# PEER gates of the first 64 tokens: accumulating indirect DMAs into a DRAM grid in place of one-hot products, in a two-block transformer step on one Trainium2 core

## The chip, the cores and the metric

The kernel runs on one core of one Trainium2 chip. The metric is the device time of one execution in microseconds. The core has five engines with instruction queues of their own: TensorE (PE in the profile; PEld is its weight load), VectorE (DVE), ScalarE (ACT), GpSimd (POOL) and SyncE (SP, which here only issues DMAs).

## What is computed

256 tokens of width 1024 pass through two blocks: a first one (gated linear attention beside sparse attention, cross attention, a PEER feed-forward), a second one (a gated recurrence beside long convolutions, a PEER feed-forward), with norms between. The change touches the PEER layer alone, which stands in both blocks:

```python
q = (xt @ wq).reshape(N, H, 2, PEER_DKEY // 2)
s = jnp.einsum('nhpd,hpkd->nhpk', q, subkeys).astype(jnp.float32)
s_half, i_half = lax.top_k(s, K)                      # 8 heads, 16 of 128 keys, twice
cand_s = (s_half[:, :, 0, :, None] + s_half[:, :, 1, None, :]).reshape(N, H, K * K)
cand_i = (i_half[:, :, 0, :, None] * PEER_NKEYS + i_half[:, :, 1, None, :]).reshape(N, H, K * K)
top_s, pos = lax.top_k(cand_s, K)
eidx = jnp.take_along_axis(cand_i, pos, axis=-1)
gate = jax.nn.softmax(top_s, axis=-1)
...
act = jax.nn.gelu(jnp.einsum('cd,chkd->chk', xc, down[ec])) * gc
y = jnp.einsum('chk,chkd->cd', act, up[ec])
```

Each token picks 8 x 16 experts of 128 x 128, and an expert's number is a pair (i, j) of key indices. The kernel does not gather experts. It computes all 16384 hidden values of all tokens, multiplies them by a gate that is zero for the experts not picked, and multiplies by all of `up`. An expert that several heads of one token pick has the sum of their gates.

## The kernel before

Matrices are streamed. `load` (244) issues one 512 KB DMA on SP's queue into one of four `wf` buffers, and `after` keeps these loads in order. `stream` (257) splits the weights: ACT copies the rounded part to `wh` (263), DVE subtracts it to get the rest, `wl` (270); both have three buffers, so they run up to three tiles ahead of PE. `mm3` (286) makes three matmuls of each pair of split operands (289 to 291). A scheduler orders each engine's instructions by readiness and by the order of the code, so DVE's order is not that of the source.

`peer` (1041) runs one PEER layer. First come the query products (`lin_t` on `wq`). `routing` (864) works on two halves of 128 tokens: the two searches for 16 keys, the search among 256 candidates, the index arithmetic, and the softmax, which ends in the multiply of line 940. Its steps are interleaved with the first 64 tiles of `down` (989), with `paced` (1032) tying them to the weight splits. One tile of `down` is 24 matmuls of 256 columns and yields the hidden values of the 128 experts of one j, for 256 tokens: row j of `H`, whose halves are `Ha` and `Hb`. ACT's gelu writes them.

The other 62 tiles (with two left for the end) are interleaved with `gate` (951), here called the gate stage. A group of four tokens takes, for each token, a one-hot matrix of its j indices times its gates (ACT, 976) and a product with the one-hot matrix of its i indices (PE, 977), which sums gates of experts picked twice. DVE multiplies the result into those columns of `H` that hold gelus already (983); where a tile of `down` comes later than the group, ACT copies the gates into `H` (985) and the tile multiplies its gelu into them (1002). DVE builds the one-hot matrices for eight tokens at a time (963). `at` is the pair that tells how many tiles and how many tokens are through.

Then `up` (1016) takes 128 pieces, one for each j: `halves` (1008) splits row j of `H` into `ah` (ACT) and `al` (DVE), in two buffers each, and 12 matmuls of 512 columns add its product with the streamed `up` weights to four accumulators.

Between the layers stands `between` (1342), a chain of residual sum, squares on ACT and two norms, whose powers are on POOL (1363). Beside it the constants of block 2 are loaded (`parts`, 427). POOL does little else: a few weight splits and products, and the powers of the norms (327).

Of the kernel before, what the change touches and what calls it, by code (L numbers as in the profile page):

```python
# [23 lines left out]
T = 256  # L24
# [3 lines left out]
NEG = -1e30  # L28
NBANK = {"lin": 3, "bank": 4, "aux": 1}
# [27 lines left out]
def _constants():  # L57
    c = {}
    c["ident"] = np.eye(P, dtype=np.float32)
    c["iota"] = np.broadcast_to(np.arange(P, dtype=np.float32), (P, P))  # L60
# [151 lines left out]
class _Kernel:  # L212
    def __init__(self, tc, ctx, A):
        self.tc, self.nc, self.A = tc, tc.nc, A
        e = ctx.enter_context
        self.pc = e(tc.tile_pool(name="const", bufs=1))
        self.px = e(tc.tile_pool(name="xs", bufs=1))
        self.pw = e(tc.tile_pool(name="w", bufs=1))
        self.ps = e(tc.tile_pool(name="ps", bufs=1, space=PSUM))
        self.dr = e(tc.tile_pool(name="dr", bufs=1, space=DRAM))  # L220
        self.small = e(tc.tile_pool(name="small", bufs=4))
        self.alt = 0
        self.last = None
        self.ahead = 3
        self.los = []

# [17 lines left out]
    def load(self, src, n):  # L244
# [4 lines left out]
        self.last = d  # L249
        return wf  # L250

# [142 lines left out]
    def setup(self):  # L394
# [4 lines left out]
        with self.tc.tile_pool(name="iota", bufs=1) as p:  # L399
            iota = self.const("iota", [P, P], pool=p)  # L400
            nc.vector.tensor_copy(self.iota, iota)
        self.mhalf = self.pc.tile([P, 1], F32, name="mhalf")
# [461 lines left out]
    def routing(self, pool, qT, sk, split_tiles, res):  # L864
# [4 lines left out]
        for i in range(2):  # L869
# [70 lines left out]
            nc.vector.tensor_tensor(out=g, in0=g, in1=sm[:, :, None].to_broadcast([P, 8, 16]), op=ALU.mult)  # L940
            b = self.bank([P, 3, P])
            for w in range(3):
                nc.tensor.transpose(b[:, w], fin[:, w].rearrange("p h k -> p (h k)"), self.ident)
# [7 lines left out]
    def gate(self, H, res, oh, at):  # L951
# [16 lines left out]
        nxt = list(hot(0))[-1]  # L968
        for t0 in range(0, T, N):
            (e, a), more = nxt, iter(hot(t0 + N)) if t0 + N < T else iter((None, None))  # L970
            for t4 in (0, 4):
# [14 lines left out]
                at[1] = t0 + t4 + 4  # L986
                yield 1

    def down(self, w, js, x, H, pool, at):
        nc = self.nc  # L990
        for j in js:
# [7 lines left out]
            if t > 0:  # L999
                g = pool.tile([P, T], F32, name="act", tag="ah")  # L1000
                nc.scalar.activation(g[:, :t], o[:, :t], AF.Gelu_apprx_tanh)
                nc.vector.tensor_tensor(out=hj[:, :t], in0=g[:, :t], in1=hj[:, :t], op=ALU.mult)
            if t < T:
                nc.scalar.activation(hj[:, t:], o[:, t:], AF.Gelu_apprx_tanh)
# [3 lines left out]
    def halves(self, hj, pool, tag, pool_lo):  # L1008

        ah = pool.tile([P, T], F32R, name="ah", tag=tag)  # L1010
# [5 lines left out]
    def up(self, w, H, pool, acc, first):  # L1016
        def piece(j):
            w2 = self.stream(w[j])
            return j, w2, first if j == 0 else self.halves(H[j // 64][:, j % 64], pool, "ah", pool)
# [21 lines left out]
    def peer(self, x, wq, nq, skname, dn, up, gain):  # L1041
        nc, A, tc = self.nc, self.A, self.tc
        with ExitStack() as st:
# [7 lines left out]
            at = [0, 0]  # L1051
            with tc.tile_pool(name="prt", bufs=1) as rp:
# [5 lines left out]
                route = self.paced(self.routing(rp, qT, sk, nq == 16, res), 1)  # L1058
# [5 lines left out]
            _interleave(self.down(A[dn], range(64, P - 2), x, H, pa, at), self.gate(H, res, oh, at), 1.02)  # L1064
            first = self.halves(H[0][:, 0], pi, "g2", pa)
# [6 lines left out]
            _run(self.up(A[up], H, pa, acc, first))  # L1072
# [319 lines left out]
    def build(self):  # L1392
        tc = self.tc
        with tc.tile_pool(name="h1", bufs=1) as ph:
# [5 lines left out]
            with tc.tile_pool(name="xap", bufs=1) as p:  # L1400
# [6 lines left out]
                self.cross(mkT, mv, self.mem_k(mc, mkT, range(6, 8)), self.mem_v(mc, mv))  # L1407
            x = self.peer_in(3)
        h, acc, g = self.peer(x, "p1_wq", 8, "p1_sk", "p1_dn", "p1_up", "nfin")
        with tc.tile_pool(name="h2", bufs=1) as ph:  # L1410
            self.h = ph.tile([P, 2, D], F32, name="hmid")
            with tc.tile_pool(name="b2n", bufs=1) as pn:
# [3 lines left out]
                self.to_cols(xn, x, range(8), lambda c: self.gains[:, 32 + c:33 + c])  # L1416
            self.block2_mix(x)
            x = self.peer_in(5)
        self.finish(*self.peer(x, "p2_wq", 16, "p2_sk", "p2_dn", "p2_up", "nfin2"))
# [22 lines left out]
```

## Time and profile before

| | |
|---|---|
| three runs, median (lowest to highest) | 2384.3 us (2381.0 to 2387.03) |
| the profiled execution, its own time | 2381.52 us |
| its span in the trace | 2379.7 us |
| mean granted clock of TensorE, share of full speed | 0.993 |
| PE, DVE, ACT, POOL busy | 98%, 71%, 54%, 3% |
| moved by DMA | 395 MB, 166 GB/s |

A line of the trace gives a start, a duration, an engine, the source line and the operation with what it writes and reads; what stands in brackets is the idle time of that engine just before and the work that ended it. PE overlaps its matmuls, so the time that one takes on PE's path is the distance of two starts, or its share in the chain of waits, and not its own duration.

### The profile page before, as it was taken

What the parts mean: (1) busy time and instruction counts of PE and PEld (TensorE: products, weight loads), DVE (VectorE), ACT (ScalarE), POOL (GpSimd) and SP (SyncE); (2) the same over time, 40 slices, a digit from 0 to 9 for tenths busy, and PEclk for the clock granted to TensorE, in tenths of its full rate; (3) what the DMA queues carried; (4) which work ended last, traced back from release to release, by engine and by line L of the source; (5) the groups of instructions that cost most, each with busy time, mean ns of one, the idle gap of its engine ahead of it and who ended that gap; (6) DMA issues with size and microseconds to landing.
All of it is one profiled execution on the core that took longest, in us unless ns stands there. A gap on an engine that the chain in (4) does not pass through costs nothing.

```text
span 2379.7 us, 40910 instructions
## 1 busy us (share of the span) xinstructions
PE 2334.1 (98%) x15646; PEld 2127.5 (89%) x15646; DVE 1686.6 (71%) x3138; ACT 1282.6 (54%) x2526; POOL 59.7 (3%) x67
## 2 busy tenths in 40 slices
PE   8999999999999999999899999999999999999998
PEld 6977889999999888888899999899999999888886
DVE  6686469886777655655778886679976777555555
ACT  6565445556777444544654434445457776444444
POOL 0002000000000000000100000200000000000000
PEclk9999999999999999999999999999999999999999
DMA  7433455564444665665554444656554444656654
GB/s 234 135 120 105 148 161 176 171 191 148 140 141 138 206 190 186 187 190 187 181 176 129 151 152 132 197 167 185 163 183 142 143 141 166 190 188 193 186 188 140
DMA packets 116084, 395.39 MB, mean 166 GB/s; under 512 B 14587, under 2 KB 21936, under 8 KB 114736
## 3 DMA queue, kind: packets, MB, share of 16 engines
q1 hardware_dynamic: 115888, 392.79, 52.7%
q8 instruction: 122, 2.00, 0.3%
q14 instruction: 74, 0.61, 0.1%
HBM read 386.45 MB, written 5.77 MB: 165 GB/s over the span
## 4 chain that ended last, share of the span: by engine, by line
PE 87%; DVE 9%; issue 1%; ACT 1%; POOL 1%; DMA 0%; POOLq 0%; SPq 0%; ACTq 0%
PE lin L291 15%; PE lin L289 15%; PE lin L290 15%; PE bank L291 10%; PE bank L289 10%; PE bank L290 10%; PE bank L977 5%; DVE wl L270 3%; PE bank L1240 1%; ACT wh L263 1%; DVE cand L906 0%; PE bank L365 0%; PE bank L655 0%; DVE pos L908 0%; PE bank L774 0%
## 5 line engine op out<-in xcount | busy, mean ns | idle before, releaser
L270 DVE TENSOR_TENSOR wl<-wf,wh 128x1024 fp32r<-128x1024 f32 (+1 forms) x698 | 852.8, 1223 | 295.7 <-ACT wh L263 295.5
L263 ACT CAST wh<-wf 128x1024 fp32r<-128x1024 f32 x704 | 735.2, 1045 | 599.0 <-PE lin L290 477.5
L289 PE MATMUL lin<-xch,wh 128*128 128x256 f32 x2912 | 839.1, 288 | 0.1
L291 PE MATMUL lin<-xch,wl 128*128 128x256 f32 x2912 | 827.5, 284 | 2.5 <-DVE wl L270 2.4
L290 PE MATMUL lin<-xcl,wh 128*128 128x256 f32 x2912 | 826.1, 284 | 0.0
L291 PEld LDWEIGHTS lin<-xch,wl 128*128 128x128 f32 x2912 | 559.1, 192 | 4.2 <-DVE wl L270 4.1
L289 PEld LDWEIGHTS lin<-xch,wh 128*128 128x128 f32 x2912 | 560.6, 193 | 2.3 <-ACT xch L375 0.7
L290 PEld LDWEIGHTS lin<-xcl,wh 128*128 128x128 f32 x2912 | 559.8, 192 | 0.0
L289 PE MATMUL bank<-wh,ah 128*128 128x512 f32 x1024 | 404.3, 395 | 0.0
L291 PE MATMUL bank<-wh,al 128*128 128x512 f32 x1024 | 404.3, 395 | 0.0
L290 PE MATMUL bank<-wl,ah 128*128 128x512 f32 x1024 | 404.2, 395 | 0.0
L291 PEld LDWEIGHTS bank<-wh,al 128*128 128x128 f32 x1024 | 192.6, 188 | 46.1
L290 PEld LDWEIGHTS bank<-wl,ah 128*128 128x128 f32 x1024 | 192.6, 188 | 45.8
L289 PEld LDWEIGHTS bank<-wh,ah 128*128 128x128 f32 x1024 | 192.6, 188 | 45.6
L976 ACT ACTIVATE c<-e,g 128x128 f32<-128x128 bf16 x512 | 175.1, 402 | 0.0
L1011 ACT CAST ah<-Hb 128x256 fp32r<-128x256 f32 x128 | 52.0, 406 | 182.4 <-PE bank L290 182.4
L1011 ACT CAST ah<-Ha 128x256 fp32r<-128x256 f32 x128 | 52.0, 406 | 177.7 <-PE bank L290 175.2
L983 DVE TENSOR_TENSOR Ha<-bank,Ha 128x256 f32<-128x256 f32 x128 | 54.2, 423 | 123.8 <-PE bank L977 119.1
L977 PE MATMUL bank<-c,a 128*128 128x128 f32 x1024 | 134.1, 274 | 0.0
L977 PEld LDWEIGHTS bank<-c,a 128*128 128x128 f32 x1024 | 124.9, 192 | 0.0
L1013 DVE TENSOR_TENSOR al<-Hb,ah 128x256 fp32r<-128x256 f32 x128 | 54.4, 425 | 78.8 <-ACT ah L1011 77.5
L1013 DVE TENSOR_TENSOR al<-Ha,ah 128x256 fp32r<-128x256 f32 x128 | 54.4, 425 | 76.0 <-ACT ah L1011 75.7
(412 smaller groups left out, 2467.2 us busy)
## 6 DMA issues: line engine op xcount, KB each, us to landing
wf<-in_p_dn_dram SPq DMA_DIRECT2D x256, 512.0 KB, 3.6
wf<-in_p_up_dram SPq DMA_DIRECT2D x256, 512.0 KB, 3.5
wf<-in_w2t_dram SPq DMA_DIRECT2D x64, 512.0 KB, 3.5
wf<-in_p_wq_dram SPq DMA_DIRECT2D x24, 512.0 KB, 3.7
wf<-in_w_out_dram SPq DMA_DIRECT2D x16, 512.0 KB, 4.2
wf<-in_w2k_dram SPq DMA_DIRECT2D x16, 512.0 KB, 3.6
wf<-in_w1t_dram SPq DMA_DIRECT2D x12, 512.0 KB, 5.0
wf<-in_w1k_dram SPq DMA_DIRECT2D x8, 512.0 KB, 3.7
```

The lines of the kernel that those rows point to most:

```text
L263: hi = self.hi = nc.scalar.copy(wh[:, :n], wf[:, :n]).ins
L270: lo = eng.tensor_tensor(out=wl[:, :n], in0=wf[:, :n], in1=wh[:, :n].bitcast(F32), op=ALU.subtract).ins
L289: mm(out, a[0], b[0], start=start, stop=False)
L290: mm(out, a[0], b[1], start=False, stop=False)
L291: self.mm = mm(out, a[1], b[0], start=False, stop=stop).ins
L976: nc.scalar.mul(c[:, x], e[:, t4 + x], gf[:, t0 + t4 + x:t0 + t4 + x + 1])
L977: nc.tensor.matmul(b[:, :, x], a[:, t4 + x], c[:, x], start=True, stop=True)
L983: nc.vector.tensor_tensor(out=hv[:, :n], in0=bv[:, :n], in1=hv[:, :n], op=ALU.mult)
L1011: self.nc.scalar.copy(ah, hj)
L1013: self.nc.vector.tensor_tensor(out=al, in0=hj, in1=ah.bitcast(F32), op=ALU.subtract)
L1240: nc.tensor.matmul(b[:, h].rearrange("p (b w m) -> p b w m", w=2, m=m), A[:, h, i * P:i * P + P], q, start=True, stop=True)
```

## The change

The 64 first tokens (`NS`) no longer take part in `gate`, which now runs from token 255 down to 64. Their gates go another way:

- `grid` makes a DRAM array of 128 x 128 x 64 numbers (i, j, token; 4 MB) for each layer. It is zeroed by eight DMAs of 512 KB from a tile of zeros, one after each of the next eight `load`s: those of the query weights for the first layer, those of the constants and first weights of block 2 for the second.
- In the first half of `routing`, two DVE operations make a table of addresses (`at`, 64 tokens x 128 picks), and `scatter` issues 128 indirect DMAs on POOL's queue, one for each pick, which add the 64 gates of this pick to the grid. Those of one head wait for all of the head before it; within a head no address repeats.
- In `up`, the grid is read back in pieces of 128 x 512 (eight j, 256 KB) on SP's queue, and `halves` multiplies the 64 columns of row j of `H` by its gates on DVE before it splits the row. The first read stands before the last two tiles of `down` in the code and waits for the last head's DMAs.
- The ratio of groups to tiles falls from 1.02 to 0.78, which spreads 48 groups over the 62 tiles.

```diff
@@ load @@
         self.last = d
+        next(self.blank, None)
         return wf
+    def grid(self, name):
+        G = self.dr.tile([P * P * NS, 1], F32, name=name)
+        v = G.rearrange("(p x) o -> p (x o)", p=P)
+        n = P * NS // 8
+        def blanks():
+            for x in range(8):
+                d = self.nc.sync.dma_start(v[:, x * n:x * n + n].rearrange("p (a t) -> p a t", t=T),
+                                           self.zero[:, None, :].to_broadcast([P, n // T, T])).ins
+                self.after(d, self.last)
+                self.last = d
+                yield x
+        self.blank = blanks()
+        return G, v
+    def scatter(self, G, at, g):
+        tc = self.tc
+        heads = self.heads[G.name] = [[]]
+        for h in range(8):
+            wait, new = heads[-1], []
+            for q in range(h * 16, h * 16 + 16):
+                d = self.nc.gpsimd.indirect_dma_start(G[:, :], bass.IndirectOffsetOnAxis(ap=at[:, q:q + 1], axis=0),
+                                                      g[0:NS, q:q + 1], None, compute_op=ALU.add).ins
+                tc.declare_no_dep(d, group=G.name, keep=wait, reason="other elements")
+                for p in wait:
+                    self.behind(d, p)
+                tc.add_to_no_dep_group(G.name, d)
+                new.append(d)
+            heads.append(new)
+    def gates(self, G, j, pool):
+        g = pool.tile([P, 8, NS], F32, name="gt")
+        d = self.nc.sync.dma_start(g.rearrange("p j t -> p (j t)"), G[1][:, j * NS:j * NS + 8 * NS]).ins
+        if j == 0:
+            for p in self.heads[G[0].name][-1]:
+                self.behind(d, p)
+        self.after(d, self.last)
+        self.last = d
+        return g
@@ routing @@
+            if i == 0:
+                at = keep.tile([NS, P], U32, name="at")
+                row = pool.tile([NS, P], F32, name="row")
+                nc.vector.tensor_scalar(row, ij[0][0:NS], float(P * NS), self.tcol[0:NS], op0=ALU.mult, op1=ALU.add)
+                nc.vector.scalar_tensor_tensor(out=at, in0=ij[1][0:NS], scalar=float(NS), in1=row, op0=ALU.mult, op1=ALU.add)
+                self.scatter(G[0], at, g)
@@ gate @@
-        nxt = list(hot(0))[-1]
-        for t0 in range(0, T, N):
+        nxt = list(hot(T - N))[-1]
+        for t0 in range(T - N, NS - 1, -N):
@@ halves @@
+        self.nc.vector.tensor_tensor(out=hj[:, :NS], in0=hj[:, :NS], in1=g, op=ALU.mult)
@@ up @@
             w2 = self.stream(w[j])
+            if j % 8 == 0 and j + 8 < P:
+                gt.append(self.gates(G, j + 8, pool))
@@ peer @@
-            _interleave(self.down(A[dn], range(64, P - 2), x, H, pa, at), self.gate(H, res, oh, at), 1.02)
-            first = self.halves(H[0][:, 0], pi, "g2", pa)
+            _interleave(self.down(A[dn], range(64, P - 2), x, H, pa, at), self.gate(H, res, oh, at), 0.78)
+            g0 = self.gates(G, 0, pa)
+            first = self.halves(H[0][:, 0], g0[:, 0], pi, "a0", pa), g0
```

Three places of the order in which the scheduler leaves the instructions. Line numbers are those of the kernel in question; in the new one 325 is the weight split (270 before), 1030 the one-hot matrices (963), 1050 the products with `H` (983), 1069 the gelus' products (1002), 1076 the new multiply, 265 a blank, 299 a read of the grid (`gt`), 250 a weight load (247).

POOL's queue from the weight splits of the first PEER layer to the powers of `between`, before:

```order
L270 TENSOR_TENSOR wl<-wf,wh 128x1024 x2
L327 TENSOR_TENSOR rstd<-rstd,mhalf 128x1 x2
L270 TENSOR_TENSOR wl<-wf,wh 128x1024
L1363 TENSOR_TENSOR ssh<-ssh,mhalf 128x1
L1363 TENSOR_TENSOR ssy<-ssy,mhalf 128x1
```

And in the changed kernel:

```order
L325 TENSOR_TENSOR wl<-wf,wh 128x1024 x2
L382 TENSOR_TENSOR rstd<-rstd,mhalf 128x1 x2
L325 TENSOR_TENSOR wl<-wf,wh 128x1024
L287 DMA gates_3161<-gn,at 1048576x1 x128
L1437 TENSOR_TENSOR ssh<-ssh,mhalf 128x1
L1437 TENSOR_TENSOR ssy<-ssy,mhalf 128x1
```

All 128 indirect DMAs of the layer stand in one run, with no other work of POOL among them.

DVE near the end of the first layer's gate stage, six tiles of `down` before the up stage, before:

```order
L983 TENSOR_TENSOR Hb_5931<-bank_8837,Hb_5931 128x58x4
L270 TENSOR_TENSOR wl_8953<-wf_8949,wh_8951 128x1024
L983 TENSOR_TENSOR Ha_3238<-bank_8886,Ha_3238 128x64x4
L1002 TENSOR_TENSOR Hb_5931<-act_8880,Hb_5931 128x236
L983 TENSOR_TENSOR Hb_5931<-bank_8886,Hb_5931 128x59x4
L963 TENSOR_TENSOR a_8934<-iotab_82,ji_3236 128x1024
L270 TENSOR_TENSOR wl_9002<-wf_8998,wh_9000 128x1024
```

And in the changed kernel (`wf_8731` and `wf_8782` hold the 122nd and 123rd down tiles, `gt_8962` the first read of the grid):

```order
L325 TENSOR_TENSOR wl_8735<-wf_8731,wh_8733 128x1024
L1069 TENSOR_TENSOR Hb_6077<-act_8627,Hb_6077 128x168
L1050 TENSOR_TENSOR Ha_3243<-bank_8670,Ha_3243 128x64x4
L1069 TENSOR_TENSOR Hb_6077<-act_8662,Hb_6077 128x168
L1050 TENSOR_TENSOR Hb_6077<-bank_8670,Hb_6077 128x56x4
L325 TENSOR_TENSOR wl_8786<-wf_8782,wh_8784 128x1024
L1076 TENSOR_TENSOR Ha_3243<-Ha_3243,gt_8962 128x64 x8
L1050 TENSOR_TENSOR Ha_3243<-bank_8719,Ha_3243 128x64x4
```

The scheduler has put the multiplies of the first eight rows of `H` together and ahead of the last products of the gate stage, so that DVE waits there for the read of the grid; on SP's queue that read stands behind the 126th down load and ahead of the last two.

SP's queue at the start of block 2, before:

```order
L247 DMA wf<-in_dft_dram 128x768 x2
L247 DMA wf<-in_idft_dram 128x256 x2
L241 DMA cw<-in_cw_dram 128x96
L1317 DMA kss<-kspec 128x256 x4
L247 DMA wf<-in_idft_dram 128x256
```

And in the changed kernel:

```order
L265 DMA gates_12116<-zero 128x4x256
L250 DMA wf<-in_idft_dram 128x256
L265 DMA gates_12116<-zero 128x4x256
L244 DMA cw<-in_cw_dram 128x96
L1391 DMA kss<-kspec 128x256 x2
L250 DMA wf<-in_idft_dram 128x256
L265 DMA gates_12116<-zero 128x4x256
```

Four blanks now stand ahead of the third `idft` load, six ahead of the first weights of block 2.

## Rows read from the trace of the kernel before

**Rows 1.** The page's first part: busy us (share of the span) xinstructions, by engine.

```profile
PE 2334.1 (98%) x15646; PEld 2127.5 (89%) x15646; DVE 1686.6 (71%) x3138; ACT 1282.6 (54%) x2526; POOL 59.7 (3%) x67
```

**Rows 2.** The page's fourth part: the chain of waits, its share of the span by engine.

```profile
PE 87%; DVE 9%; issue 1%; ACT 1%; POOL 1%; DMA 0%; POOLq 0%; SPq 0%; ACTq 0%
```

**Rows 3.** Table by stretches: us, busy PE, PEld, DVE, ACT, POOL (instructions), PEclk, DMA share, GB/s.

```profile
350.00:500.00 150.00, 148.79 (x1237) 147.37 (x1236) 141.28 (x426) 74.73 (x117) 0.00 (x0) 1.00 0.55 170
545.00:745.00 200.00, 200.00 (x1702) 200.00 (x1701) 146.93 (x266) 145.84 (x428) 0.00 (x0) 1.00 0.46 140
800.00:1120.00 320.00, 320.00 (x1373) 257.42 (x1372) 189.53 (x235) 157.09 (x232) 0.00 (x0) 1.00 0.61 188
1126.00:1150.00 24.00, 18.78 (x80) 14.58 (x78) 17.75 (x37) 14.64 (x35) 3.06 (x4) 0.91 0.47 145
1653.00:1740.00 87.00, 86.71 (x726) 86.51 (x725) 79.69 (x240) 42.87 (x70) 0.00 (x0) 1.00 0.55 171
```

**Rows 4.** The chain in routing, 372 to 390 us: start us, us, what.

```profile
381.67 1.13 DVE wl L270
...
384.78 1.13 DVE wl L270
```

**Rows 5.** The chain in the gate stage, 745 to 755 us.

```profile
745.64 0.89 PE bank L977 x8
...
749.41 0.89 PE bank L977 x8
```

**Rows 6.** Costliest groups: line engine op xcount | busy, mean ns | idle before.

```profile
L263 ACT CAST wh<-wf 128x1024 fp32r<-128x1024 f32 x704 | 735.2, 1045 | 599.0 <-PE lin L290 477.5
...
L977 PE MATMUL bank<-c,a 128*128 128x128 f32 x1024 | 134.1, 274 | 0.0
```

**Rows 7.** DVE by time in the gate stage: start us, us, what [idle before <-releaser].

```profile
742.80 0.42 DVE L983 TENSOR_TENSOR Ha<-bank,Ha 128x256 f32<-128x256 f32 x1 [1.64 <-PE bank L977]
```

**Rows 8.** DVE by time in routing, both PEER layers.

```profile
402.49 0.22 DVE L919 TENSOR_SCALAR pu<-pos 128x128 uint32<-128x128 uint32 x1
...
421.61 0.29 DVE L940 TENSOR_TENSOR fin<-fin,gsm 128x128 f32<-128x128 f32 x1
...
1652.65 0.29 DVE L940 TENSOR_TENSOR fin<-fin,gsm 128x128 f32<-128x128 f32 x1
```

**Rows 9.** POOL by time, 1143 to 1530 us.

```profile
1143.17 0.93 POOL L1363 TENSOR_TENSOR ssh<-ssh,mhalf 128x1 f32<-128x1 f32 x1 [815.07 <-DVE ssh L1359]
...
1488.43 4.12 POOL L1115 TENSOR_TENSOR mg<-mg,yb 128x256 f32<-128x256 f32 x3 [1.50 <-DVE yb L1114]
...
1494.67 0.74 POOL L1115 TENSOR_TENSOR mg<-mg,yb 128x256 f32<-128x256 f32 x1 [2.11 <-DVE yb L1114]
...
1528.19 0.56 POOL L327 TENSOR_TENSOR rstd<-rstd,mhalf 128x1 f32<-128x1 f32 x1 [0.33 <-DVE rstd L326]
```

**Rows 10.** SP's DMA queue by time, where the up loads begin, both layers.

```profile
763.91 5.20 SPq L247 DMA_DIRECT2D wf<-in_p_up_dram  x2
...
1995.36 16.05 SPq L247 DMA_DIRECT2D wf<-in_p_up_dram  x5
```

**Rows 11.** DMA issues: out<-in engine op xcount, KB each, median us to landing.

```profile
wf<-in_p_dn_dram SPq DMA_DIRECT2D x256, 512.0 KB, 3.6
...
kss<-kspec SPq DMA_DIRECT2D x24, 128.0 KB, 2.3
...
kspec<-spec SPq DMA_DIRECT2D x8, 256.0 KB, 2.1
```

**Rows 12.** DVE by time beside POOL's multiplies, 1485 to 1506 us.

```profile
1495.06 1.42 DVE L270 TENSOR_TENSOR wl<-wf,wh 128x1024 fp32r<-128x1024 f32 x1 [0.47 <-ACT wh L263]
```

**Rows 13.** ACT by time at the start of block 2.

```profile
1141.81 0.41 ACT L433 CAST idfth<-wf 128x256 fp32r<-128x256 f32 x1 [0.74 <-DMA wf<-in_idft_dram]
```

**Rows 14.** DVE by time in the up stage.

```profile
789.14 0.42 DVE L1013 TENSOR_TENSOR al<-Ha,ah 128x256 fp32r<-128x256 f32 x1 [0.61 <-ACT ah L1011]
...
790.09 1.23 DVE L270 TENSOR_TENSOR wl<-wf,wh 128x1024 fp32r<-128x1024 f32 x1 [0.53 <-ACT wh L263]
```

More of the change, by code (lines that the diff above doesn't have):

```diff
@@ L225, in __init__ @@
         self.los = []
+        self.blank, self.heads = iter(()), {}
     def bank(self, shape, tag="bank"):
@@ L401, in setup @@
             nc.vector.tensor_copy(self.iota, iota)
+        self.tcol = self.const("tcol", [P, 1])
+        self.zero = self.pc.tile([P, T], F32, name="zero")
+        nc.gpsimd.memset(self.zero, 0.0)
         self.mhalf = self.pc.tile([P, 1], F32, name="mhalf")
@@ L860, in cross, with routing @@
             _run(self.lin_k(A["xa_wo"], range(2), cat, self.residual))
-    def routing(self, pool, qT, sk, split_tiles, res):
+    def routing(self, pool, qT, sk, split_tiles, res, keep, G):
         nc = self.nc
@@ L939, in routing @@
             nc.vector.reciprocal(sm, sm)
-            nc.vector.tensor_tensor(out=g, in0=g, in1=sm[:, :, None].to_broadcast([P, 8, 16]), op=ALU.mult)
+            gn = g if i else keep.tile([P, 8, 16], F32, name="gn")
+            nc.vector.tensor_tensor(out=gn, in0=g, in1=sm[:, :, None].to_broadcast([P, 8, 16]), op=ALU.mult)
+            ij, g = [fin[:, w].rearrange("p h k -> p (h k)") for w in range(2)], gn.rearrange("p h k -> p (h k)")
+            if i == 0:
[4 more added lines that the diff above has]
+                self.scatter(G[0], at, g)
             b = self.bank([P, 3, P])
             for w in range(3):
-                nc.tensor.transpose(b[:, w], fin[:, w].rearrange("p h k -> p (h k)"), self.ident)
+                nc.tensor.transpose(b[:, w], (*ij, g)[w], self.ident)
             s = slice(i * P, i * P + P)
@@ L966, in hot @@
                 yield e, a
-        nxt = list(hot(0))[-1]
-        for t0 in range(0, T, N):
-            (e, a), more = nxt, iter(hot(t0 + N)) if t0 + N < T else iter((None, None))
-            for t4 in (0, 4):
+        nxt = list(hot(T - N))[-1]
+        for t0 in range(T - N, NS - 1, -N):
+            (e, a), more = nxt, iter(hot(t0 - N)) if t0 > NS else iter((None, None))
+            for t4 in (4, 0):
                 nxt = next(more)
@@ L1039, in paced, with peer @@
             yield v
-    def peer(self, x, wq, nq, skname, dn, up, gain):
+    def peer(self, x, wq, nq, skname, dn, up, gain, G):
         nc, A, tc = self.nc, self.A, self.tc
@@ L1071, in peer @@
             nc.sync.dma_start(g, A[gain])
-            _run(self.up(A[up], H, pa, acc, first))
+            _run(self.up(A[up], H, G, pa, acc, first))
         return h, acc, g
```

35 lines of the change are left out of this document (22 added, 13 removed).

## The prediction

> **What bounds the kernel now.** I read the page's first part first. TensorE (PE) is busy 98% of the span, VectorE (DVE) 71%, ScalarE (ACT) 54%, GpSimd (POOL) 3% [rows 1]. A busy share can hide a wait, so the chain of waits comes next: PE holds 87% of it and DVE 9% [rows 2]. The table by stretches tells where each of them counts [rows 3]. From 545 to 745 us (the gate stage of the first PEER layer) and from 800 to 1120 (its up stage) PE is busy for the whole stretch; DVE has 27% and 41% of it free. From 350 to 500 and from 1653 to 1740 (routing beside the first half of the down stage) DVE is busy 94% and 92%. There the chain runs through DVE: its weight splits stand 3.11 us apart [rows 4], where a down tile alone takes PE 2.88 [rows 5]. So PE work taken out of the gate stage comes off the end; DVE work put into routing goes onto it; DVE work put into the up stage has room.
>
> **What is removed.** A group of four tokens costs PE 0.89 us of the chain, and groups stand 3.77 us apart, with a tile of 2.88 between [rows 5]. Line 977 has 1024 records, two for each of 512 tokens [rows 6], so 128 groups. The order of the program shows 96 in the new one, 32 fewer. 32 x 0.89 = **28.5 us** off, 14.2 per layer. The other engines do not take over: in the gate stage DVE stands still 1.6 us for PE every second tile [rows 7], and each tile keeps at most one group. The one-hot builds, ACT's scalings and the products with H of these tokens go too; they lie beside PE and are worth nothing.
>
> **What is added.** Five things.
>
> First, DVE in routing: two operations on 64x128 per layer that make the addresses. The nearest rows are 0.22 us (128x128, one input) and 0.29 (128x128, two inputs) [rows 8], so some 0.45 per layer on the path: **0.9 us**. The normalised gates merely go to another tile.
>
> Second, the 128 accumulating DMAs per layer on POOL's queue. Nothing on POOL waits behind them: its next work after the first layer's is at 1143 us, after 815 us of idling [rows 9]. Who waits is SP's queue, which holds the first read of the grid behind the 126th down load, and DVE, which has the first eight multiplies behind the 123rd weight split. The gates of the first 128 tokens are ready at 421.9 [rows 8]. The first up load is issued at 763.91 [rows 10]; the 126th down load is three loads of 3.77 us earlier, about 753, and 14 us earlier once the groups are gone: 739. So the DMAs have 317 us. The eight heads each end with a full wait. The nearest such wait is a small load's 2.3 us [rows 11], 8 x 2.3 = 18, and **2.33 us per DMA** is the point from which the read comes late. No row of before shows an indirect DMA. From below, POOL's smallest operation is 0.56 us [rows 9]; from above, that plus a full landing of 2.3 with nothing overlapped is 2.9. I take 1.5, on the lower side, since the code lets eight be in flight: 128 x 1.5 + 18 = 210 us, done at about 632, a hundred before the read. Cost 0; at the upper end it is the third rival. The second layer has the same room: its gates are ready at 1652.9 [rows 8] and its first up load goes out at 1995.36 [rows 10], both 1231 us later.
>
> Third, what POOL does to DVE meanwhile. Beside a POOL multiply DVE's weight split takes 1.42 us [rows 12] instead of 1.23 [rows 14], and three POOL multiplies beside DVE take 4.12 us instead of 3 x 0.74 [rows 9]. Each delays the other. DVE is on the path only until routing ends, about 80 us per layer, in which 50 DMAs go out at 1.5 us. Costs of 0 to 0.2 us each give 0 to 20 us for both layers. An address column is far shorter than a multiply's 128x256, so I take 0.045: **4.5 us**. A gain is excluded, as DVE's own work there does not shrink.
>
> Fourth, plain traffic on SP's queue. Eight blanks of 512 KB per layer: a 256 KB store to DRAM lands after 2.1 us [rows 11], so a blank needs up to 3.6. In the first layer they lie between loads of the query weights, four buffers ahead, and I cost them at nothing; without that cover they would cost what they cost at the second. In the second they stand between the small loads at the start of block 2, where ACT already waits 0.74 us for one of these loads, on the way to the next norm [rows 13]. Four blanks stand ahead of that load. The DMA engines are at 47% there, so most fits in gaps: 0 to 8 us, I take **2**. Sixteen reads of 256 KB per layer raise the up stage's traffic by a sixteenth of 4 MB over its 64 MB; its DMA share is 0.61 [rows 3]. Cost 0.
>
> Fifth, again on DVE, 256 multiplies of 128x64 in the up stage, at most 0.29 us each. DVE idles 0.61 and 0.53 us in each of the 256 pieces [rows 14], four times as much. One batch of eight, 2.3 us at most, comes while splits are a piece ahead. Cost 0. The first read: issued behind a load that lands 3.6 us later [rows 11], it lands about 4.5 after the 122nd split frees its buffer, while DVE comes to the multiplies one tile (3.77) after that split. DVE stands a microsecond. The split that it holds back has 5 us in hand: with three buffers a split is wanted two tiles (7.5 us) after its buffer came free, less ACT's cast of 1.05 [rows 6] and its own 1.2. Cost 0.
>
> **The sum.** The profiled execution took 2381.5 us (span 2379.7). 2381.5 - 28.5 + 0.9 + 4.5 + 2 = 2360.4. The median of the three runs is 2.8 above it, which would make 2363. I say **2361**.
>
> [...] The rows show DVE and POOL delaying each other by 0.2 and 0.63 us per operation [rows 9, 12]. [...]
>
> **The rivals.**
> 1. *Given back in routing.* The same mechanism, with DVE and the DMAs at the upper bounds: 0.2 us for each of 100 DMAs is 20, the blanks 8. 2381.5 - 28.5 + 0.9 + 20 + 8 = 2382, no change. For it: DVE is at 92 to 94% there and on the chain. Against: the descriptors need one short column each.
> 2. *The change doesn't do what it says:* it leaves the groups or lets ACT and DVE set the tile. The order shows 96 groups, and DVE's idle time shows room. If tiles without a group ran at 3.11 as in routing, 28 such tiles would cost 7 us: 2367, inside my range.
> 3. *The scatter is late (slower).* Each DMA waits for DVE's operation under way, 1.5 + 1.2 = 2.7 us, above the deciding 2.33. 128 x 2.7 + 18 = 364 us, 47 after the read is due. SP's queue then holds every later weight, and DVE every later split; PE has about 5 us in hand. 42 us per layer: 2360 + 84 = **2444**. At 2.5 us it is 2360 + 2 x 16 = 2393. For it: each POOL operation beside DVE took 1.37 us instead of 0.74, and read-add-write may be slower than any row here. Against: eight in flight, and 317 us of room.
>
> **How the numbers follow.** About 0.3% (7 us) is what a measurement of this kernel can tell from no change. My forecast, DMAs in time and 12 to 31 us gained, has 0.69 (with rival 2, some 0.04, inside). Rival 1, within 7 us of before, 0.11. Slower is rival 3, 0.19, and 0.01 for a sum of small delays. So faster 0.69, same 0.11, slower 0.20. The range begins at 2350 (the full 28.5 and a few us of runs) and must take in rival 1 and the near end of rival 3, up to 2400, leaving out some 0.16 above and 0.03 below. The forecast's own range is 2350 to 2370.
>
> **What would show it.** Right: 96 groups on PE, still 0.89 us each; no new wait of PE or DVE for a DMA longer than some us near the end of the gate stage; POOL's last accumulate well before SP's first read of the grid; routing splits still about 3.1 us apart. Wrong: the read of the grid or the first multiply waits tens of us and PE idles there (rival 3); the stretch from routing's first half to its end grows by 10 us a layer, with longer splits (rival 1); or PE waits near the start of block 2 for a load behind the blanks.

## The result

| | before | changed | ratio, 95% interval |
|---|---|---|---|
| median of the runs | 2383.6 us | 2356.7 us (2354.3 to 2360.2) | 0.9888 [0.9876, 0.9900] |
| span of the profiled execution | 2379.7 us | 2354.2 us | |

The changed kernel is 26.9 us faster; the forecast was 2361. The page of the changed kernel, parts 1 and 4 (answers to [rows 1, 2]):

```profile
PE 2307.6 (98%) x15390; PEld 2100.5 (89%) x15390; DVE 1675.5 (71%) x3300; ACT 1240.8 (53%) x2368; POOL 471.6 (20%) x324
...
PE 90%; DVE 7%; issue 1%; ACT 1%; POOL 1%; DMA 0%; POOLq 0%; SPq 0%; ACTq 0%
```

PE lost 256 instructions (64 tokens, 2 records, 2 layers) and 26.5 us; POOL went from 60 to 472 us. The same stretches as in [rows 3], moved with the program:

```profile
350.00:500.00 150.00, 148.79 (x1236) 147.36 (x1235) 138.14 (x429) 72.73 (x108) 59.01 (x38) 1.00 0.61 169
545.00:735.00 190.00, 190.00 (x1611) 190.00 (x1610) 129.50 (x227) 128.40 (x362) 114.15 (x70) 1.00 0.56 149
800.00:1110.00 310.00, 310.00 (x1330) 249.38 (x1329) 197.32 (x332) 151.54 (x224) 0.00 (x0) 1.00 0.63 199
1114.00:1138.00 24.00, 18.05 (x78) 13.79 (x76) 17.84 (x39) 15.39 (x35) 3.05 (x4) 0.90 0.82 259
1640.00:1727.00 87.00, 86.67 (x725) 86.47 (x724) 76.47 (x240) 39.74 (x61) 66.43 (x43) 1.00 0.67 173
```

PE is as full as before in the stages of routing, gates and up. At the start of block 2 (fourth line) it has 18.05 us instead of 18.78, and the DMA share rose there from 0.47 to 0.82. A group still costs what it did [rows 5], in the chain of the gate stage:

```profile
727.97 0.89 PE bank L1044 x8
...
731.74 0.89 PE bank L1044 x8
```

To see where the time went, I cut the span at four PE instructions: the first score product of each layer's routing (lines 884 and 880 of before, 942 and 938 now) and the last one-hot product of each gate stage (977, 1044). "Up 1, block 2" is then the first layer's up stage and block 2 as far as the second routing, and "rest" is the second up stage and the end. Lengths in us, worked out from the starts of these instructions in each trace; the kernels below the second are the experiments:

| kernel | to first score | routing and gates 1 | up 1, block 2 | routing and gates 2 | rest |
|---|---|---|---|---|---|
| before | 341.4 | 435.9 | 785.3 | 446.1 | 371.0 |
| changed | 342.7 | 421.8 | 785.9 | 432.0 | 371.8 |
| noscat | 343.6 | 421.8 | 786.1 | 432.0 | 372.5 |
| addonly | 341.4 | 436.0 | 785.1 | 446.2 | 373.1 |
| dve20 | 343.5 | 421.8 | 786.4 | 432.0 | 371.7 |
| dve80 | 347.1 | 427.7 | 785.0 | 437.3 | 371.6 |
| late | 343.5 | 421.8 | 786.1 | 432.0 | 373.2 |
| heads4 | 342.8 | 433.1 | 784.7 | 440.0 | 371.8 |
| heads2 | 343.4 | 505.4 | 786.2 | 517.0 | 373.2 |
| ns96 | 346.5 | 414.9 | 784.9 | 424.9 | 371.7 |
| ns128 | 341.0 | 410.1 | 789.5 | 417.8 | 371.7 |
| mv64 | 346.6 | 422.1 | 784.5 | 432.0 | 371.3 |
| mv128 | 344.2 | 410.2 | 786.2 | 418.1 | 371.3 |
| best | 343.6 | 407.7 | 786.3 | 418.0 | 371.3 |

The change took 14.1 us from each layer's routing and gates, 28.2 together, and gave back 2.6 elsewhere in this execution: 1.3, 0.6 and 0.7 in the other three columns.

Two of these columns hold a spread of their own. In every kernel of the table the products of an up stage take either 356.7 or 358.15 us from first to last (357.3 once), with PE waiting for nothing (0.33 us in that one); before and the changed kernel have 358.15 in the first layer and 356.7 in the second. So 1.45 us in "up 1, block 2" or "rest" need not come from the change.

The scatter, POOL's accumulating DMAs by line (duration ns min/median/max, first and last start; then what POOL sat idle for: us, times):

```profile
L287 POOL DMA_INDIRECT gates<-gn,at x256: 1390/1407/2433, 423.6 to 1902.2; - x128
...
  issue: 72.2, 237
  DMA gates<-gn,at: 48.1, 17
```

```profile
691.63 1.40 POOL L287 DMA_INDIRECT gates<-gn,at  x1 [0.30 <-issue]
...
1902.19 1.60 POOL L287 DMA_INDIRECT gates<-gn,at  x1 [0.30 <-issue]
```

The page has 411.6 us busy for the 256, so 1.61 us each, and 0.30 between two. Of the 17 idle times put down to a DMA three are such gaps of 0.30; the other 14, one behind each head but the last of a layer, make 47.2 us, 3.4 for a full wait. The first layer's 128 last from 423.6 to 693.0, 269 us. SP's queue by time shows the first reads of the grid:

```profile
742.15 0.33 SPq L299 DMA_DIRECT2D gt<-gates  x1
...
1960.10 0.33 SPq L299 DMA_DIRECT2D gt<-gates  x1
```

They go out 49 and 56 us after the last accumulate. VectorE stands for the first of them, but not for long:

```profile
745.49 1.18 DVE L1076 TENSOR_TENSOR Ha<-Ha,gt 128x64 f32<-128x64 f32 x8 [0.31 <-DMA gt<-gates]
```

Why a DMA takes POOL 1.41 us in the median and up to 2.43, a long one shows beside VectorE's operation at its start:

```profile
566.20 2.43 POOL L287 DMA_INDIRECT gates<-gn,at  x1 [0.30 <-issue]
```

```profile
566.14 1.22 DVE L325 TENSOR_TENSOR wl<-wf,wh 128x1024 fp32r<-128x1024 f32 x1
```

The DMA ends 1.27 us after the split does. 95 of the 256 took over 1.5 us, and 93 of them end 1.27 to 1.30 us after a VectorE operation on two tensors, neither of them a result of PE, that ran when they began, 80 times a weight split. Of the 97 DMAs that began with 0.23 us or more of such an operation still to run, 95 are long; of the 24 that began so beside a search, a reduction or a product that reads a result of PE, none is. So the DMA waits until that operation ends, which makes some 53 us for all 256.

ACT's wait for the load that has four blanks ahead of it at the start of block 2 [rows 13] has not grown; what the blanks cost there is found under mv64:

```profile
1128.89 0.40 ACT L491 CAST idfth<-wf 128x256 fp32r<-128x256 f32 x1 [0.62 <-DMA wf<-in_idft_dram]
```

The up stage's DVE rows [rows 14] are nearly unchanged:

```profile
781.93 0.43 DVE L1080 TENSOR_TENSOR al<-Ha,ah 128x256 fp32r<-128x256 f32 x1 [0.62 <-ACT ah L1078]
782.88 1.23 DVE L325 TENSOR_TENSOR wl<-wf,wh 128x1024 fp32r<-128x1024 f32 x1 [0.52 <-ACT wh L318]
```

### The profile page after: what moved, and what is told of

Its sections match the earlier page's. It is cut to its first block, busy times and chain, and to the rows that moved or that the text cites. A ratio compares the mean times of both kernels' runs of the same rounds, so it can differ in the third digit from the quotient of the medians.

```text
span 2354.2 us, 40890 instructions
## 1 busy us (share of the span) xinstructions
PE 2307.6 (98%) x15390; PEld 2100.5 (89%) x15390; DVE 1675.5 (71%) x3300; ACT 1240.8 (53%) x2368; POOL 471.6 (20%) x324
## 4 chain that ended last, share of the span: by engine, by line
PE 90%; DVE 7%; issue 1%; ACT 1%; POOL 1%; DMA 0%; POOLq 0%; SPq 0%; ACTq 0%
PE lin L346 16%; PE lin L344 16%; PE lin L345 16%; PE bank L346 11%; PE bank L344 11%; PE bank L345 10%; PE bank L1044 4%; DVE wl L325 2%; PE bank L1314 1%; PE bank L420 1%; PE bank L713 0%; ACT wh L318 0%; PE bank L832 0%; DVE cand L964 0%; POOL rstd L382 0%
## 5 line engine op out<-in xcount | busy, mean ns | idle before, releaser
L287 POOL DMA_INDIRECT gates<-gn,at x256 | 411.6, 1608 | 329.1 <-DVE gn L999 114.4
L382 POOL TENSOR_TENSOR rstd<-rstd,mhalf 128x1 f32<-128x1 f32 (+1 forms) x18 | 13.3, 741 | 802.4 <-DVE rstd L381 737.2
L1043 ACT ACTIVATE c<-e,g 128x128 f32<-128x128 bf16 x384 | 132.7, 402 | 0.0
L1050 DVE TENSOR_TENSOR Ha<-bank,Ha 128x256 f32<-128x256 f32 x96 | 40.8, 425 | 104.6 <-PE bank L1044 102.4
```

The source lines that it names most:

```text
L287: d = self.nc.gpsimd.indirect_dma_start(G[:, :], bass.IndirectOffsetOnAxis(ap=at[:, q:q + 1], axis=0), g[0:NS, q:q + 1], None, compute_op= ...
L1043: nc.scalar.mul(c[:, x], e[:, t4 + x], gf[:, t0 + t4 + x:t0 + t4 + x + 1])
L1050: nc.vector.tensor_tensor(out=hv[:, :n], in0=bv[:, :n], in1=hv[:, :n], op=ALU.mult)
```

## The experiments

The theory after the result is A in the expectations (B and C are the rivals that each of them names): only PE's time of the removed groups counts, and the additions are free while the scatter is in time. The rivals are the prediction's own costs in routing, and a gain that comes from something else. All medians stand beside 2383 us for before and 2356.7 for the changed kernel.

**Without the DMAs (noscat).**

```diff
-                self.scatter(G[0], at, g)
+                self.heads[G[0].name] = [[]]
```

> The changed kernel without its 256 indirect DMAs; blanks, address arithmetic, reads and multiplies stay, so the gates of the first 64 tokens are left out (zero). Theory A (from the trace of the changed kernel: down tiles in the routing stretch start as far apart as before, so POOL writing descriptors costs VectorE nothing that TensorE sees): the time of the changed kernel, 2356.7, within 1 us. Rival B (the prediction's step on POOL and VectorE side by side in routing, +4.5 us): 2352. Rival C (the scatter's end is awaited somewhere although the first read was issued 50 us after it): lower by more than 10 us.

Measured: 2358.1 us, 0.9897 [0.9882, 0.9912]; routing and gates as long as with the DMAs to 0.1 us. The 256 DMAs cost nothing. VectorE's operations beside them were no longer either; its searches from 430 to 550 us with the scatter, and then without (POOL waits for VectorE, but VectorE not for POOL):

```profile
L946 DVE FIND_INDEX8 ix<-v,ssb 128x8 uint32<-128x128 f32 x16 | 4.6, 285 | 0.0
```

```profile
L946 DVE FIND_INDEX8 ix<-v,ssb 128x8 uint32<-128x128 f32 x16 | 4.6, 290 | 0.0
```

**All added, nothing removed (addonly).**

```diff
-        for t0 in range(T - N, NS - 1, -N):
+        for t0 in range(T - N, -1, -N):
...
-            _interleave(self.down(A[dn], range(64, P - 2), x, H, pa, at), self.gate(H, res, oh, at), 0.78)
+            _interleave(self.down(A[dn], range(64, P - 2), x, H, pa, at), self.gate(H, res, oh, at), 1.02)
```

> Everything the change adds, and nothing it removes: all 64 groups of one-hot products per layer again (ratio 1.02 as before), and also blanks, scatter, reads and multiplies; the first 64 tokens get their gate twice. Theory A: the saving is the 32 groups' TensorE time alone (28.3 us) and the additions cost 1.4 (start) + 0.2 (routing) + 0.8 (start of block 2), so the time is before's plus about 2.4: 2386. Rival B (the prediction's sum of costs, 0.9 + 4.5 + 2): before's plus 7.4: 2391. Rival C (a part of the gain comes from the groups' reversed order or from the other use of ScalarE, not from the removed products): below before's, by up to 10 us.

Measured: 2386.1 us, 1.001 [1.0001, 1.0019]. Both layers' routing and gates are before's to 0.1 us. So the reversed order gains nothing and the additions cost nothing there; the removal alone is worth 28.3 us (14.1 and 14.2 against the changed kernel), 0.885 per group. The 2.6 us by which the median is above before's agree with A in size, but not by its parts: the way to the first score is 341.4 as in before, and the excess stands in the last column, 1.45 us of it as the longer of the up stage's two lengths.

**More VectorE work in routing (dve20, dve80).**

```diff
                 row = pool.tile([NS, P], F32, name="row")
+                for _ in range(20):
+                    nc.vector.tensor_scalar(row, ij[0][0:NS], float(P * NS), self.tcol[0:NS], op0=ALU.mult, op1=ALU.add)
```

> The changed kernel with the first of the two address operations (0.22 us on VectorE in the profile of before) done 20 more times in each layer's routing, 8.8 us of VectorE in all, the result the same. Rival B (the prediction's step: VectorE's work put into routing lies on the path): plus 8.8, 2365.5. Theory A (weight splits of VectorE run ahead of TensorE there, so 4.4 us in one place are absorbed): at most plus 0.5, 2357.

Measured: 2358.3 us, 0.9895 [0.9880, 0.9910]; both layers' routing and gates unchanged. Nothing is paid of the added operations, which in the trace take 5.2 us a layer. VectorE by time in the changed kernel shows why:

```profile
422.53 0.27 DVE L1005 TENSOR_SCALAR row<-fin,tcol 64x128 f32<-64x128 f32 x1
...
422.84 0.28 DVE L1006 SCALAR_TENSOR_TENSOR at<-fin,row 64x128 uint32<-64x128 f32 x1
...
427.41 1.22 DVE L325 TENSOR_TENSOR wl<-wf,wh 128x1024 fp32r<-128x1024 f32 x1 [1.65 <-ACT wh L318]
429.66 0.76 DVE L1014 CAST ji<-bank 128x256 bf16<-128x256 f32 x2 [1.03 <-PE bank L1010]
...
433.49 1.22 DVE L325 TENSOR_TENSOR wl<-wf,wh 128x1024 fp32r<-128x1024 f32 x1 [1.75 <-ACT wh L318]
```

Right behind the address operations VectorE stands still for 1.65 + 1.03 + 1.75 = 4.4 us, between the two halves of routing. The stage is 92% busy there on average, but not in this place. In dve20's trace the added operations stand there, among the splits, and VectorE has no idle time from 423 to 436 us.

> The changed kernel with the first address operation done 80 more times in each layer's routing (17.6 us of VectorE in one piece, 35 us in all); 20 more cost TensorE nothing. Theory A (VectorE's splits stand ahead of TensorE by some tiles, and VectorE makes up the rest of its delay later in the stage, so only what goes beyond the lead is paid): between 0 and 2 x 10 us, 2357 to 2377. Rival B (VectorE is not needed there at all in time): 2357. Rival C (the prediction's step, every us of VectorE in routing is paid): 2392.

Measured (the same loop with 80): 2370.2 us, 0.9947 [0.9930, 0.9964]. Routing and gates grew by 5.9 and 5.3 us; the 80 operations take 16.8 us a layer in the trace, so some 11 are absorbed. VectorE's work is paid once the gaps and the lead of the splits are used up. PE by time has one stand in the first layer, and the table by stretches (columns as in [rows 3]) what follows it:

```profile
451.80 0.58 PE L346 MATMUL lin<-xch,wl 128*128 128x256 f32 x1 [3.29 <-DVE wl L325]
```

```profile
444.00:448.00 4.00, 4.00 (x34) 3.87 (x33) 4.00 (x25) 2.02 (x3) 0.00 (x0) 1.00 0.19 77
448.00:452.00 4.00, 0.71 (x5) 0.52 (x5) 4.00 (x20) 0.64 (x2) 0.00 (x0) 0.92 0.00 0
452.00:456.00 4.00, 4.00 (x24) 4.00 (x24) 4.00 (x19) 0.09 (x1) 0.00 (x0) 0.65 0.39 131
456.00:460.00 4.00, 4.00 (x31) 3.61 (x31) 4.00 (x20) 2.10 (x4) 0.00 (x0) 1.00 0.62 142
```

PE stood 3.29 us but lost 5.9. A part of the rest is its clock: the granted clock was 0.92 of full speed in the 4 us of the stand and 0.65 in the next 4; behind the stand one matmul starts after 381 ns and 12 after 213, where the matmuls ahead of it start every 120, which makes 1.4 us. In the second layer PE stood 3.06 us and lost 5.3, and there the first distance of 380 and 25 of 213, together 2.6 us, cover the rest. In the first layer some 1.2 us stay unexplained.

**The start (late).**

```diff
-        self.tcol = self.const("tcol", [P, 1])
-        self.zero = self.pc.tile([P, T], F32, name="zero")
-        nc.gpsimd.memset(self.zero, 0.0)
...
+            self.tcol = self.const("tcol", [P, 1])
+            self.zero = self.pc.tile([P, T], F32, name="zero")
+            self.nc.gpsimd.memset(self.zero, 0.0)
             G = self.grid("gates1")
```

> The changed kernel with the load of the token column and the clearing of the zero tile moved from the program's start to just before the first grid is declared (some 300 us later). Theory A (the 1.4 us that TensorE is later from the first 120 us on come from these two): minus 1.4, 2355.3. Rival B (that shift is only the span's origin, or another placement): 2356.7 unchanged.

Measured: 2358.9 us, 0.9895 [0.9880, 0.9910]; 343.5 us to the first score instead of 342.7. A falls. This column lies between 341.0 and 347.1 over the kernels of the table, and addonly, with the same additions at the start, has before's 341.4: what the changed kernel seemed to lose there is the spread of single executions. The granted clock goes with it: from 100 to 200 us it is 0.98 on average in before and addonly, 0.93 in the six kernels between 343.4 and 344.2, and 0.90 in the three between 346.5 and 347.1.

**A later scatter (heads4, heads2).** A full wait after every 4, or 2, DMAs instead of 16.

```diff
-        for h in range(8):
+        for h in range(32):
...
-            for q in range(h * 16, h * 16 + 16):
+            for q in range(h * 4, h * 4 + 4):
```

> The changed kernel with a full wait of the scatter after each 4 DMAs instead of each 16: 32 waits of 2.8 us a layer instead of 8, the rest of the scatter 247 us: 247 + 32 x 2.8 = 338 us in a room of about 317. Theory A (the prediction's third rival: when the scatter is late, TensorE stands until the grid is read, in full): late by some 20 us in each layer, 2356.7 + 40 = 2397, of which some may be lower since SP's first reading may land 1 to 3 us earlier than needed. Rival B (shorter batches make each wait shorter, since it is the queue's draining): 2357.

> The changed kernel with a full wait of the scatter after each 2 DMAs: 64 waits of 2.8 us: 247 + 64 x 2.8 = 426 us a layer in a room of about 317. Theory A (a late scatter costs TensorE its whole lateness): 109 us in each layer, 2356.7 + 218 = 2575. Rival B (a shorter wait per batch, 1 us): 311 us, still in time: 2357.

Measured: 2374.2 us, 0.997 [0.9945, 0.9994], and 2531.4, 1.0625 [1.0601, 1.0649]. SP's waits (us in total, times, longest), first of heads4, then of heads2:

```profile
SPq L299 <- DMA gates<-gn,at: 25.9, 4, 13.2
```

```profile
SPq L299 <- DMA gates<-gn,at: 175.9, 2, 88.4
```

heads4 is 11.3 and 8.0 us later in routing and gates (19.3 of SP's 25.9), heads2 83.6 and 85.0 (168.6 of 175.9). So a late scatter is paid in full but for 3 to 4 us a layer. Theory A's mechanism holds. Its sizes were too high: it reckoned with 247 us a layer beside the waits, and the first layers have 236 in heads4 and 220 in heads2, since a full wait stands in the place of a gap of 0.30 and is not added to it. The waits were 3.1 us (190.6 / 62) and 2.9 (364.7 / 125) beside 3.4 with batches of 16, not the 1 us of B, so B falls. In heads2 the chain of causes reads, VectorE, then PE, then the table by stretches:

```profile
832.78 1.17 DVE L1076 TENSOR_TENSOR Ha<-Ha,gt 128x64 f32<-128x64 f32 x8 [86.92 <-DMA gt<-gates]
```

```profile
835.40 0.79 PE L1044 MATMUL bank<-c,a 128*128 128x128 f32 x2 [80.60 <-ACT c L1043]
837.16 0.58 PE L346 MATMUL lin<-xch,wl 128*128 128x256 f32 x1 [0.53 <-DVE wl L325]
```

```profile
834.00:838.00 4.00, 2.06 (x8) 1.77 (x9) 4.00 (x9) 2.62 (x8) 0.00 (x0) 0.50 0.00 0
838.00:842.00 4.00, 4.00 (x26) 4.00 (x26) 3.25 (x5) 3.54 (x11) 0.00 (x0) 0.68 0.74 218
842.00:846.00 4.00, 4.00 (x37) 4.00 (x36) 2.22 (x9) 2.23 (x6) 0.00 (x0) 1.00 0.64 241
```

VectorE holds the multiplies by the read `gt`, and with them the one-hot builds and splits behind them; PE stands 81.1 us (80.60 + 0.53) and the first layer loses 83.6. The 2.5 us more go, as in dve80's second layer, to the clock: the granted clock is 0.50 of full speed in the stretch in which PE starts again, and 0.68 in the 4 us after, and 2.6 us at 0.50 and 4 at 0.68 make a loss of 2.6 by an estimate from these numbers.

**More tokens (ns96, ns128).**

```diff
-NS = 64
+NS = 128
...
-            _interleave(self.down(A[dn], range(64, P - 2), x, H, pa, at), self.gate(H, res, oh, at), 0.78)
+            _interleave(self.down(A[dn], range(64, P - 2), x, H, pa, at), self.gate(H, res, oh, at), 0.52)
```

> The changed kernel with the first 96 tokens by scatter instead of 64 (128 DMAs per layer of 96 elements, grid of 6 MB, 40 groups per layer left, ratio 0.65). Theory A (TensorE's time of the removed groups is all that counts while the scatter is in time): 16 groups less x 0.89 = minus 14.2: 2342.5, if a DMA of 96 elements, with waits, stays under (317 - 7) / 128 = 2.4 us (2.1 us with 64 elements). Rival B (POOL's time goes with the elements: 1.6 x 1.5 + 0.3 + 0.2 = 2.9 us per DMA): the scatter is 61 us late in each layer, 2342.5 + 122 = 2465.

> The changed kernel with all 128 tokens of the first routing half by scatter (128 DMAs per layer of 128 elements, grid of 8 MB, 32 groups per layer left, ratio 0.52). Theory A (a DMA's time hardly goes with its elements): 32 groups less x 0.89 = minus 28.4: 2328.3. Rival B (POOL's time goes with the elements: 1.6 x 2 + 0.3 + 0.2 = 3.7 us per DMA, 474 us in a room of 317 - 14): late by 170 us in each layer, about 2670.

Measured: 2342.5 us, 0.9824 [0.9804, 0.9843], and 2335.3, 0.9798 [0.9778, 0.9818]. The first is A's number (2342.5). The DMAs' durations, first with 96 tokens, then with 128:

```profile
L287 POOL DMA_INDIRECT gates<-gn,at x256: 1404/1416/2472, 427.2 to 1901.0; - x128
```

```profile
L287 POOL DMA_INDIRECT gates<-gn,at x256: 1539/1558/2594, 424.1 to 1918.9; - x128
```

Elements hardly count: the mean is 1.61 us with 64 and with 96, 1.81 with 128. With 128 tokens 7 us of A's gain are missing. The first table shows where: 3.6 us more than the changed kernel in "up 1, block 2", and routing and gates of the first layer 11.7 us shorter instead of 14.2. Both are places of the blanks, which are now 1 MB each.

**Blanks moved (mv128, mv64, best).** The second grid is declared before the first layer's up stage and cleared in 32 pieces, one behind every third load; best also declares the first grid before the cross attention, in 32 pieces, one behind every load.

```diff
-        n = P * NS // 8
+        n = P * NS // pieces
...
-            for x in range(8):
+            for x in range(pieces):
+                for _ in range(every - 1):
+                    yield x
...
+            self.G = self.grid("gates2", 32, 3) if up == "p1_up" else None
             _run(self.up(A[up], H, G, pa, acc, first))
...
-            G = self.grid("gates2")
```

And in best alone:

```diff
+                G = self.grid("gates1", 32, 1)
                 self.cross(mkT, mv, self.mem_k(mc, mkT, range(6, 8)), self.mem_v(mc, mv))
-            G = self.grid("gates1")
```

> The kernel with 128 tokens by scatter, the second grid declared before the first layer's up stage and cleared in 32 pieces of 256 KB, one behind every third weight load there, instead of 8 pieces of 1 MB behind the first loads of block 2. Theory A (in the trace of the kernel with 128 tokens TensorE loses 3.7 us against the kernel before in the first 15 us of block 2, where the blanks stand between weight loads): minus 3.7 from 2335.3: 2331.6. Rival B (the blanks then delay weight loads of the up stage as much): 2335, with the loss between 760 and 1130 us of the span. Rival C (the loss at block 2's start is not the blanks'): 2335, with the loss still there.

Measured: 2330.5 us, 0.9778 [0.9762, 0.9794]; "up 1, block 2" fell from 789.5 to 786.2. The 1110 to 1140 us stretch of ns128, and then of mv128 (whose block 2 starts 3.2 us later; from 1113.2 to 1143.2 us PE's time in it is the same 22.32):

```profile
1110.00:1140.00 30.00, 19.73 (x108) 16.39 (x107) 22.54 (x51) 19.38 (x42) 3.63 (x5) 0.77 1.00 348
```

```profile
1110.00:1140.00 30.00, 22.32 (x111) 18.40 (x110) 22.93 (x51) 20.25 (x43) 3.06 (x4) 0.77 0.54 172
```

The blanks had filled the DMA engines (share 1.00, 348 GB/s) just where block 2 waits for its first weights. From the up stage's last product to the second layer's first score, ns128 takes 426.9 us and mv128 423.6.

> The changed kernel (64 tokens) with the second grid's blanks moved in the same way (32 pieces of 128 KB in the first layer's up stage). Theory A: TensorE's loss of 1.0 us at the start of block 2 goes: 2356.7 - 1 = 2355.7, and in the trace the first weight tile of block 2 comes no later behind the up stage than in the kernel before. Rival B: no difference there.

Measured: 2354.6 us, 0.988 [0.9863, 0.9896], not apart from the changed kernel by time. "Up 1, block 2" is 1.4 us shorter, but kernels with the same blanks there range from 784.7 to 786.4, mostly by the two lengths of the up stage. Without that stage the answer is clear: from its last product to the second layer's first score, before and mv64 take 421.3 us, and the eight kernels with eight blanks of 512 KB there 421.9 to 422.5. PE's first matmul on weights of block 2 starts 10.5 us behind that product in before, 11.5 in the changed kernel and 10.6 in mv64. So the blanks cost 0.6 to 1.2 us, and A holds.

> The kernel with 128 tokens by scatter and both grids cleared in 32 pieces of 256 KB: the second in the first layer's up stage (as in the run before), the first declared before the cross attention, so that its pieces stand behind that part's weight loads, instead of 8 pieces of 1 MB behind the first loads of the first PEER layer. Theory A (in the trace with 128 tokens TensorE loses 2.7 to 3.0 us against the changed kernel between 347 and 360 us of the span, where these blanks stand): minus 2.5 from 2330.5: 2328. Rival B (pieces of 256 KB cost the cross attention's loads as much as they cost these): 2330.5.

Measured: **2328.4 us**, 0.9775 [0.9761, 0.9789], the fastest kernel of this study; routing and gates of the first layer fell from 410.2 to 407.7, as A has it (from the medians alone mv128 and best can't be told apart). Elements and places of the blanks aside, 128 tokens have a loss that A has not: from the up stage's last product to the second first score mv128 and best take 423.6 and 423.8 us where mv64 takes 421.3. ACT casts the first weight tile there 11.2 us behind that product in mv128 and 9.5 in mv64, with its operations in another order; no run tests whether the order is the cause. Now both layers' routing and gates are 28 us shorter than before's. The stretch in ns128 and in best:

```profile
335.00:365.00 30.00, 27.72 (x216) 26.36 (x215) 24.88 (x110) 13.14 (x18) 0.00 (x0) 0.94 0.67 234
```

```profile
335.00:365.00 30.00, 28.93 (x240) 28.09 (x239) 23.61 (x101) 14.57 (x20) 0.00 (x0) 1.00 0.52 170
```

PE stands 1.2 us less in best, and its granted clock is 1.00 instead of 0.94.

## Why the prediction was right, and where it was off

- **What is removed, 28.5 us: right.** The trace has 28.2 for the 32 groups, addonly 28.3. It was a count of groups times a distance of PE starts in a stage where PE is busy throughout [rows 3, 5].
- **"DVE work put into routing goes onto" the path: wrong as a rule for the stage**, and with it the step that charged 0.9 us for two address operations. dve20 put in more than ten times as much and paid nothing. The prediction joined a share over 150 us (VectorE 94% busy) with a chain that runs through VectorE from 372 to 390 us [rows 4], and did not follow the chain to the place of the new operations, behind 421 us. From the list of the chain's longest pieces in before, three that follow each other:

```profile
412.21 1.23 DVE wl L270
431.20 1.64 PE bank L884 x16
455.99 1.05 ACT wh L263
```

Piece by piece the chain runs through PE alone from 413.49 to 455.96, and in the second layer from 1639.34 to 1729. PE's 148.79 us of 150 [rows 3] say the same: it hardly waited for VectorE. dve80 shows how far the slack goes: of 16.8 us in one place PE waits for 3.3, and with the clock's share 5.9 are paid.
- **POOL beside DVE, 4.5 us (0 to 20): mis-sized, at 0.** noscat takes the DMAs away and routing and gates do not change by 0.1 us. Two tensor operations slow each other (1.37 us instead of 0.74 on POOL, 1.42 instead of 1.23 on VectorE) [rows 9, 12]; beside these DMAs only POOL waits: VectorE's splits from 430 to 550 us take 1.22 us each with and without them. The two steps make 5.4 us and the forecast was 4.3 too high, so they cover the miss; the rest of the account is the 2.6 us given back, of which the prediction had 2 as blanks.
- **The scatter, 210 us in a room of 317: in time, but mis-sized.** It took 269 us: 1.91 us per DMA with the gap, not 1.5, and 3.4 per full wait, not 2.3. The reason given for 1.5, eight DMAs in flight, does not show: POOL starts the next 1.9 us after one, and the 32 of ns96 that have a landing in the trace land 2.7 to 5.5 us after their start, so by an estimate from these two or three were under way. The room was right (318.5 from the first DMA at 423.6 to the read at 742.15; the forecast had the read at 739), and so was the cost of 0. The margin was half of what was thought: 49 us, or 0.38 us per DMA. That the scatter was in time was in part luck.
- **VectorE's delay of a DMA, 1.2 us in the third rival: right in kind, too high.** With VectorE busy for most of the time (129.5 us of 190 from 545 to 735), the mean of POOL's time per DMA is 1.61 us and the longest 2.43. 95 of the 97 DMAs that began well before the end of a VectorE operation on two tensors, neither a result of PE, were held up, by 0.1 to 1.03 us, while the 24 that began so beside other operations were not. So the third rival's "each DMA waits for DVE's operation under way" is what happens, but to 95 of 256 and for the rest of the operation only: 0.21 us in the mean, not 1.2.
- **Blanks, 2 us at block 2: the right place, about half the size.** With 512 KB they cost 0.6 to 1.2 us there (mv64) and nothing in the first layer, where addonly's routing and gates are before's to 0.1 us; with 1 MB they cost 3.3 and 2.5 (mv128, best).
- **Reads and multiplies in the up stage, 0: right.** PE is busy 310 of 310 us there. VectorE stood 0.31 us for the first read, where a microsecond was forecast, and PE did not.
- **Rivals 1 and 2** fall: routing and gates became 14.1 us shorter a layer and not 10 longer, and PE has the products of 96 groups, 768 instead of 1024.
- **Rival 3** had the mechanism right: heads2 is that case, at 85 us late a layer. In heads4 and heads2 PE stands 6.1 to 6.5 us less than SP waits for the scatter, so it had that much in hand, where 5 was forecast; behind the stand 2.5 to 3.1 us are lost again, so that 3 to 4 remain.

Of the 2.6 us outside routing and gates, the 0.6 in "up 1, block 2" are the blanks, and the 1.3 before the first score lie within the spread. What stays open are the 0.7 us behind the second up stage's last product, where the table's kernels lie between 8.5 and 9.2 us, and why the up stage has two lengths.

## What to carry to other kernels

Here work taken from an engine that was busy throughout a stage came off the end one for one (28.5 us by count, 28.2 in the trace); work added beside it was free as long as its last result landed before the queue that needs it got there (269 us of DMAs in a room of 318), and a late one was paid in full but for 3 to 4 us a layer. So work out that room, and price the time per instruction with its gap (1.91 us here) and the full waits between batches (3.4). A busy share of 94% over a stage did not put an added operation on the path (5.2 us a layer in dve20 cost nothing): follow the chain to the very place, and look at the idle time there and at whether the engine that sets the end has any. Bulk stores in front of the first loads of a stage held up PE (eight of 1 MB cost 3.3 us at block 2, eight of 512 KB 0.6 to 1.2); cut in 32 pieces and spread over a stage with room they cost nothing that showed: from the up stage's last product to the next layer's first score, before and mv64 take 421.3 us.

## What was not expected of the hardware

- An accumulating indirect DMA cost POOL nearly the same for 64, 96 and 128 elements: median 1.41, 1.42 and 1.56 us, plus 0.30 to the next.
- Such a DMA waited for the VectorE operation on two tensors, neither a result of PE, that ran when it began, up to 1.03 us (95 of 97), but in the changed kernel for no other operation (none of 24); VectorE did not wait for the DMA (285 ns for a search with the DMAs, 290 without).
- A full wait for such DMAs took about 3 us whether 16, 4 or 2 were in the batch (3.4, 3.1, 2.9).
- Behind a stand of 3.3 us, and one of 81 us, PE's granted clock was down at 0.65 and 0.50; it was 1.00 again in the stretches that begin 4.2 and 6.6 us after PE's restart. Over the six stands of dve80, heads4 and heads2, from 3 to 82 us long, the loss beyond PE's idle time was 2.2 to 3.1 us: 2.6 behind the stand of 3.3 us, 2.5 behind that of 81.
- The same 1536 matmuls of an up stage took 356.7 or 358.15 us, with no wait of PE in them and at a granted clock of 1.00.
